# A mixture-of-experts layer: the transposes of a tail's second gated half move behind the main block's down product, and one of the two down weight groups is split into two reduced-precision halves

## The chip, the cores and the metric

The kernel runs on one core of a Trainium2 chip. The metric is the time of one execution in microseconds (us) as the device gives it, the median of several runs. The core has a matrix engine (TensorE, "PE" in the rows, "PEld" its weight loads), a vector engine (VectorE, "DVE"), an activation engine (ScalarE, "ACT"), GpSimd ("POOL") and a queue of transfers ("SP"). Each engine works off its own list of instructions in order, and they wait for each other by semaphores.

## The reference, cut to what matters

The layer is a decoder block: layer norm and modulation, attention and pooling, an output projection, and then a mixture of 16 experts, of which every token uses two. The change touches the experts alone:

```python
def hierarchical_moe(u, w_rg, b_rg, w_re, b_re, w_gate, w_up, w_down):
    ...
    y = jnp.zeros((t, d), jnp.float32)
    for e in range(N_EXPERTS):
        h = jax.nn.silu(u @ w_gate[e]) * (u @ w_up[e])
        y = y + combine[:, e:e + 1] * (h @ w_down[e]).astype(jnp.float32)
    return y.astype(u.dtype)
```

There are 1024 tokens, the model width is 1024 and an expert's hidden width is 512. All is float32.

## The kernel before, in words

The first 560 us are the attention half and the routing. Then the 16 experts follow one another in the program, numbered here by their place, 0 to 15. An expert gathers its tokens by an indirect transfer (`gather`): up to 128 in the main block, and if it has more than 128, up to 64 in a **tail**. Everything for the tail stands in two branches on the count (`tc.If(n_e > P)`, lines 1242 and 1263), which every engine takes or skips by itself. With the inputs at hand the experts at places 2, 4, 6, 8, 10 and 12 have a tail.

The weights of an expert come in six groups of 1 MB, 128 x 4 x 512 float32 (`load_group`): groups 0 and 1 are the first half of the gate and up weights, 2 and 3 the second half, 4 and 5 the down weights. They land in a ring of eleven buffers (`RAW`, whose names in the rows are `raw`, `arena`, `mixT`). For the main block, groups 0 to 3 are **split** (`split_group`): ACT rounds a half group to a reduced-precision float32 (`HR`, line 968) and DVE takes the remainder (`LR`, line 971), two halves per group, into a ring of three slots (`NH`). The tokens are split in the same way (`prep`: PE transposes them at line 998, ACT makes the high part at line 1000, DVE the low part at line 1001, both named `xa`). A product of split operands is three PE passes, high by high, high by low, low by high (`mm_split`, lines 1091 to 1093). `NSP = 4` is the number of groups per expert that are split. As soon as group s has been used, the splitting of group s + 3 is issued.

The main block of an expert: `gate_up(0)` and `gate_up(1)` are 48 passes. Each gives a 128 x 512 sum of gate and up, which `gated` turns into 256 hidden columns (ACT line 1148, DVE line 1149). `turn` transposes these on PE (two transposes, line 1156) and ACT copies them out of PSUM to `hh` (line 1158). The first half a0 is turned in the midst of `gate_up(1)`, the second half a1 after the first branch. `down` multiplies `hh` by the down weights as plain float32, eight matmuls of 128 x 512 (line 1175). `emit` scales the result and `send` adds it to a buffer in memory by an indirect transfer (line 1224).

The tail, in the first branch: its tokens are transposed and copied (`xb`, lines 1007 and 1008), 16 plain float32 matmuls per half on two halves of the array (`gate_up_tail`, line 1097), then `fold` (ACT line 1011, DVE line 1012) and `gated` for the halves b0 and b1, and `turn` for both. The second branch holds the tail's down product and its `emit`.

After the first branch the tokens of the next expert are prepared (`prep(e + 1)`). The transposes of `prep` and of `turn` share two PSUM buffers, `tr`, in turn. A scheduler orders the instructions of each engine, so that the lists of the engines differ somewhat from the order of the source and from expert to expert. The end is the last expert together with a final layer norm (`final`) over the buffer in memory, which can be read only when expert 14 has sent its result.

Of the kernel before, what the change touches and what calls it, by code (L numbers as in the profile page):

```python
# [8 lines left out]
F32 = mybir.dt.float32  # L9
F32R = mybir.dt.float32r  # L10
BF16 = mybir.dt.bfloat16
I32 = mybir.dt.int32
AF = mybir.ActivationFunctionType
# [4 lines left out]
P = 128  # L18
# [3 lines left out]
KC = D // P  # L22
# [8 lines left out]
NE = 16  # L31
NCH = 24
GRP = 4
# [17 lines left out]
WS = "vvvv"  # L51
PRE = 0
SPLIT = 800
NSP = 4
RB = 0
TB = 1
MT = 2
# [28 lines left out]
def row_bcast(ap, n, off=0):  # L86
    return bass.AP(tensor=ap.tensor, offset=ap.offset + off, ap=[[0, P], [1, n]])
# [3 lines left out]
def hybrid_layer(ctx: ExitStack, tc: tile.TileContext, x, c, w_ada, b_ada, w_qk, w_v, w_p, w_pool,  # L91
                 pool_scale, w_out, ln1_g, ln1_b, w_r, b_r, w_moe, ln2_g, ln2_b, eye, out):
    nc = tc.nc
# [35 lines left out]
    def after(a, b, c=mybir.DependencyClass.NoSync):  # L129
        tc.add_manual_dep(b.ins, a.ins.name, mybir.DependencyInfo(c, mybir.DependencyReason.DATA), reason="order")  # L130
# [16 lines left out]
    if True:  # L147
# [369 lines left out]
        for t in range(nfill):  # L517
# [6 lines left out]
            while done < acc:  # L524
                n = next(fill, None)
# [8 lines left out]
        pt = ps.tile([P, 512], F32, name="tr")  # L534
# [18 lines left out]
    g1, b1, sc2, h2, gate1 = (rows[:, r] for r in range(5))  # L553
# [311 lines left out]
    NL, NH = 11, 3  # L865
# [84 lines left out]
    act = moe.enter_context(tc.tile_pool(name="act", bufs=2))  # L950
# [8 lines left out]
    def note(k, ins):  # L959
        newest[k] = ins  # L960
        return ins

    def split_group(s):
        m = NG * (s // NSP) + s % NSP
        r, l, h = RAW[m % NL], LR[s % NH], HR[s % NH]
        for a in range(2):
            cs = slice(2 * a, 2 * a + 2)
            rnd = note("a", nc.scalar.activation(h[:, cs], r[:, cs], AF.Copy))  # L968
            if s == 0:
                after(turned[0], rnd)  # L970
            sub = note("d", nc.vector.tensor_sub(l[:, cs], r[:, cs], h[:, cs]))  # L971
            if s < NH:
                after(ready, sub)
# [3 lines left out]
    def slots(e, b, n):  # L977
        if e < NS:
            return Ti[:n, b * 16 + e, 0:1], T[:n, b * 16 + e, 1:2]
        return TP.bitcast(I32)[:n, b, e - NS, 0:1], TP[:n, b, e - NS, 1:2]  # L980
# [22 lines left out]
    def prep_tail():  # L1003
        for g in range(2):
            pt = ps.tile([P, 4, HB], F32, name="tr")
            for j in range(4):
                nc.tensor.transpose(pt[:, j], XG[2][:HB, (4 * g + j) * P:(4 * g + j + 1) * P], ident[:HB, :HB])
            note("a", nc.scalar.activation(xb[:, 4 * g:4 * g + 4], pt, AF.Copy))
# [63 lines left out]
    def expert(e, n_e):  # L1072
# [9 lines left out]
        xa_h, xa_l = XA[e % 2]  # L1082
        hts = [[], []]

        def raw(g, j):
            return RAW[(NG * e + g) % NL][:, j]

        def mm_split(o, k, s, j):
            tick()
            h, l = HR[s % NH][:, j], LR[s % NH][:, j]  # L1090
            nc.tensor.matmul(o, xa_h[:, k], h, start=k == 0, stop=False)  # L1091
            nc.tensor.matmul(o, xa_h[:, k], l, start=False, stop=False)  # L1092
            nc.tensor.matmul(o, xa_l[:, k], h, start=False, stop=k == KC - 1)  # L1093

        def mm_pair(o, x, w, k, n):
            q = HALF[k % 2]
            nc.tensor.matmul(o[q], x, w, start=k < 2, stop=k >= n - 2)

        def whole_of_ybuf(ins):
            for o in sent[-1]:  # L1100
                after(o, ins, mybir.DependencyClass.Sync)

        def rest(t):
            if not last:
                return
            if t == 0:
                nc.sync.dma_start(gb[:, 0], row_bcast(ln2_g, D))
                nc.sync.dma_start(gb[:, 1], row_bcast(ln2_b, D))
                for i in range(NT):
                    whole_of_ybuf(nc.sync.dma_start(YT[i], ybuf[i * P:(i + 1) * P]))  # L1110
            if t == 1:
                for b in range(2):
                    whole_of_ybuf(nc.gpsimd.indirect_dma_start(
                        out=XG[2 if b else e % 2][:cnts[b]], out_offset=None, in_=ybuf[:],
                        in_offset=bass.IndirectOffsetOnAxis(ap=slots(e, b, cnts[b])[0], axis=0),
                        bounds_check=S - 1, oob_is_err=False))
# [3 lines left out]
        def tick():  # L1120
            ticks[0] += 1
            n = ticks[0] - BS1
            if last and n >= 0 and n % BR1 == 0:
                next(bulk, None)

        def gate_up(half, mid=None):
            pg = ps.tile([P, 512], F32, name="mm", bufs=6)
            for k in range(KC):
                s = NSP * e + 2 * half + k // GRP
                mm_split(pg, k, s, k % GRP)  # L1130
                if mid and k in mid:
                    mid[k]()
                if k % GRP == GRP - 1 and s + NH < NE * NSP:
                    split_group(s + NH)
            return pg

        def gate_up_tail(half):
            pg = ps.tile([P, 512], F32, name="mm", bufs=6)
            for k in range(KC):
                mm_pair(pg, xb[:, k], raw(2 * half + k // GRP, k % GRP), k, KC)  # L1140
            return pg

        def gated(b, pg):
            n = cnts[b]
            s = act.tile([P, 512], F32, name="silut" if b else "silu")[:n]
            if n == HB:
                pg = fold(s, pg)
            note("a", nc.scalar.activation(s[:, :256], pg[:, :256], AF.Silu))
            note("d", nc.vector.tensor_mul(s[:, :256], s[:, :256], pg[:, 256:]))
            return s  # L1150

        def turn(b, s):
            n = cnts[b]
            pt = ps.tile([P, 2, P], F32, name="tr")
            for j in range(2):
                nc.tensor.transpose(pt[:, j, :n], s[:, j * P:(j + 1) * P], ident[:n, :n])
            hh = act.tile([P, 2, P], F32, name="hh", bufs=4)[:, :, :n]
            note("a", nc.scalar.activation(hh, pt[:, :, :n], AF.Copy))
            hts[b].append(hh)

        pys = [[], []]
# [3 lines left out]
        def down(b, g):  # L1165
            for dh in range(2):
                if g == 0:
                    pys[b].append(ps.tile([P, 512], F32, name="mm", bufs=6))
                for f in range(2):
                    k, w = 2 * g + f, raw(4 + g, 2 * f + dh)  # L1170
                    if b:
                        mm_pair(pys[b][dh], hts[b][g][:, f], w, k, 4)
                    else:
                        tick()
                        nc.tensor.matmul(pys[b][dh], hts[b][g][:, f], w, start=k == 0, stop=k == 3)  # L1175
# [4 lines left out]
        def new_y(b):  # L1180
            ys_[b] = ytail if b else act.tile([P, D], F32, name="y", bufs=1)
# [40 lines left out]
        def send(b):  # L1222
            n = cnts[b]
            sc = nc.gpsimd.indirect_dma_start(  # L1224
                out=out if last else ybuf[:], out_offset=bass.IndirectOffsetOnAxis(ap=slots(e, b, n)[0], axis=0),
                in_=ys_[b][:n], in_offset=None, bounds_check=S - 1, oob_is_err=False,
                **({} if last else dict(compute_op=OP.add)))
            for o in stores if last else ():
                after(o, sc, mybir.DependencyClass.Sync)
            for o in sent[-1]:  # L1230
                after(o, sc, mybir.DependencyClass.Sync)
            for o in prev:
                tc.declare_no_dep(sc.ins, o.ins, reason="tokens of one expert are distinct")
            prev.append(sc)

        rest(0)
        pa0 = gate_up(0)
        a0 = gated(0, pa0)
        rest(1)
        pa1 = gate_up(1, {MT: lambda: turn(0, a0)})  # L1240
        a1 = gated(0, pa1)
        with tc.If(n_e > P):
            prep_tail()
            pb0 = gate_up_tail(0)
            b0 = gated(1, pb0)
            pb1 = gate_up_tail(1)
            turn(1, b0)
            b1 = gated(1, pb1)
            turn(1, b1)
        newest.clear()  # L1250
        refill(range(NG * e, NG * e + 4))
        if not last:
            prep(e + 1)
        turn(0, a1)
        down(0, 0)
        down(0, 1)
        new_y(1)
        new_y(0)
# [2 lines left out]
        emit(0)  # L1261
        send(0)
        with tc.If(n_e > P):
            down(1, 0)
            down(1, 1)
            emit(1)
# [5 lines left out]
    def refill(ms):  # L1272
        for m in ms:
            if m + NL < NE * NG:
                load_group(m + NL)
# [64 lines left out]
    with tc.If(top > P + HB):  # L1340
# [8 lines left out]
        e = nc.values_load(perm[0:1, ND - 1:ND], min_val=0, max_val=NE - 1)  # L1349
# [63 lines left out]
```

## Time and profile before

| | us |
|---|---|
| three runs | 1035.01 to 1038.65, median 1037.75 |
| the profiled execution, its own time | 1037.95 |
| its span, from the first to the last instruction | 1036.2 |
| PE busy | 866.7 (84%) |
| DVE busy | 724.6 (70%) |
| ACT busy | 463.3 (45%) |
| mean granted TensorE clock | 0.924 of 2.4 GHz |

Outside the span lie 1.75 us. PE is the busiest engine, but a share of busy time is a mean over stages; the stage that the change touches runs from 567 to 988 us. Matmuls are recorded longer than their distance, since they are pipelined: what a pass costs is read from the starts of the records. A plain float32 matmul leaves two records in the trace, a split pass or a transpose one.

### The profile page before, as it was taken

The page shows a single profiled execution, that of the slowest core. Times are in us where ns is not written, and L with a number is a line of the kernel's source. Part 1 is how long each engine was busy: PE and PEld are TensorE (multiplying, and loading weights), DVE is VectorE, ACT ScalarE, POOL GpSimd, SP SyncE. Part 2 cuts the span into 40 slices and gives each one's busy share as a digit, 9 for nine tenths or more (in the row PEclk, how much of TensorE's full clock was granted, in tenths as well). Part 3 has the DMA queues.
Part 4 walks back from the last instruction along what each step waited for, and adds up shares of the span by engine and source line. Part 5 has one row for each costly group of instructions (what it writes and reads, how often), then busy time and mean ns, then how long its engine had stood idle before and what let it go on. Part 6 is the DMA issues. An engine that isn't in the chain of part 4 may idle for free. (4 is left out here: it accounts for less than half of the span.)

```text
span 1036.2 us, 12860 instructions
## 1 busy us (share of the span) xinstructions
PE 866.7 (84%) x4109; PEld 594.7 (57%) x4110; DVE 724.6 (70%) x1249; ACT 463.3 (45%) x792; POOL 357.7 (35%) x356
## 2 busy tenths in 40 slices
PE   4879888999989798879763999989898999999820
PEld 3658666777767566666642664636455555546510
DVE  7889899787888896968486664735565655647453
ACT  3341544545545654555223553634444544535260
POOL 4775052060134334445463421203020211211383
PEclk7899989999999898999885999999999999999965
DMA  8847533010100522224237697968768787787741
GB/s 307 302 145 247 193 102 102 24 41 24 42 23 21 153 92 82 83 77 174 95 130 293 237 341 251 304 220 269 278 197 322 211 310 222 282 281 265 231 177 63
DMA packets 42467, 186.90 MB, mean 180 GB/s; under 512 B 7921, under 2 KB 8977, under 8 KB 30096
## 3 DMA queue, kind: packets, MB, share of 16 engines
q1 hardware_dynamic: 34608, 168.57, 44.9%
q0 software_dynamic: 7776, 17.33, 7.2%
q8 instruction: 40, 0.66, 0.3%
q14 instruction: 43, 0.35, 0.1%
HBM read 169.19 MB, written 25.33 MB: 188 GB/s over the span
## 5 line engine op out<-in xcount | busy, mean ns | idle before, releaser
L1091 PE MATMUL mm<-HR,xa 128*128 128x512 f32 x256 | 106.9, 418 | 0.1
L988 POOL DMA_INDIRECT V<-u2d,TP x28 | 33.9, 1212 | 209.5 <-issue 85.5
L1092 PE MATMUL mm<-LR,xa 128*128 128x512 f32 x256 | 102.2, 399 | 0.1
L1093 PE MATMUL mm<-HR,xa 128*128 128x512 f32 x256 | 100.4, 393 | 0.1
L971 DVE TENSOR_TENSOR LR<-raw,HR 128x1024 fp32r<-128x1024 f32 x56 | 68.4, 1224 | 19.6 <-ACT HR L968 16.8
L968 ACT ACTIVATE HR<-raw 128x1024 fp32r<-128x1024 f32 x56 | 59.3, 1061 | 49.2 <-PE mm L1093 48.8
L422 PE MATMUL mm<-AT,V 128*64 128x128 f32 x576 | 60.2, 313 | 24.1 <-ACT AT L413 11.6
L971 DVE TENSOR_TENSOR LR<-mixT,HR 128x1024 fp32r<-128x1024 f32 x50 | 61.1, 1224 | 18.7 <-ACT HR L968 15.6
L968 ACT ACTIVATE HR<-mixT 128x1024 fp32r<-128x1024 f32 x50 | 53.0, 1061 | 45.9 <-PE mm L1093 45.7
L471 PE MATMUL mm<-uh,wh 128*128 128x512 f32 x160 | 70.9, 443 | 3.1 <-ACT V L315 1.9
L473 PE MATMUL mm<-uh,wl 128*128 128x512 f32 x160 | 65.4, 409 | 1.9 <-DVE wl L170 1.9
L422 PEld LDWEIGHTS mm<-AT,V 128*64 128x64 f32 x576 | 42.2, 154 | 42.9 <-ACT AT L413 16.8
L472 PE MATMUL mm<-ul,wh 128*128 128x512 f32 x160 | 65.0, 406 | 0.0
L383 DVE TENSOR_TENSOR_SCAN N<-N,zcol 128x767 f32<-128x767 f32 (+7 forms) x45 | 59.4, 1321 | 6.7 <-ACT N L377 6.2
L444 POOL TENSOR_TENSOR mixT<-pT 128x344 f32<-128x344 f32 (+1 forms) x12 | 14.3, 1204 | 131.2 <-ACT pT L432 131.2
L1175 PE MATMUL mm<-raw,hh 128*128 128x512 f32 x112 | 58.1, 650 | 0.4
L1091 PEld LDWEIGHTS mm<-HR,xa 128*128 128x128 f32 x256 | 48.6, 190 | 13.9 <-issue 3.3
L1092 PEld LDWEIGHTS mm<-LR,xa 128*128 128x128 f32 x256 | 48.6, 190 | 13.2 <-issue 4.1
L1093 PEld LDWEIGHTS mm<-HR,xa 128*128 128x128 f32 x256 | 48.4, 189 | 10.6 <-issue 0.8
L410 PE MATMUL tr<-ident,arena 128*128 128x128 f32 x288 | 46.2, 284 | 8.0 <-DVE L L728 6.2
L1220 DVE SCALAR_TENSOR_TENSOR y<-mm,TP,sg 128x512 f32<-128x512 f32 x26 | 19.5, 750 | 38.4 <-PE mm L1175 35.7
L377 ACT ACTIVATE N<-zz 128x767 f32<-128x767 f32 (+7 forms) x45 | 28.2, 627 | 39.1 <-DVE zz L376 38.8
(375 smaller groups left out, 2226.2 us busy)
## 6 DMA issues: line engine op xcount, KB each, us to landing
raw<-in_w_moe_dram SPq DMA_DIRECT2D x42, 1024.0 KB, 7.7
mixT<-in_w_moe_dram SPq DMA_DIRECT2D x36, 1024.0 KB, 8.8
arena<-in_w_moe_dram SPq DMA_DIRECT2D x18, 1024.0 KB, 7.8
arena<-in_w_ada_dram SPq DMA_DIRECT2D x24, 512.0 KB, 4.3
wada<-in_w_ada_dram SPq DMA_DIRECT2D x12, 512.0 KB, 5.9
mixT<-in_w_ada_dram SPq DMA_DIRECT2D x12, 512.0 KB, 3.5
ybuf<-sg SPq DMA_DIRECT2D x8, 512.0 KB, 2.6
wraw<-in_w_qk_dram SPq DMA_DIRECT2D x6, 512.0 KB, 4.0
```

The costliest lines, as they stand in the source:

```text
L383: nc.vector.tensor_tensor_scan(N[:, 1:nk], N[:, 1:nk], zcol.to_broadcast([P, nk - 1]), 1.0, op0=OP.mult, op1=OP.add)
L410: nc.tensor.transpose(pt[:, j], E[:, (g + j) * P:(g + j + 1) * P], ident)
L422: nc.tensor.matmul(po[h * HD:(h + 1) * HD, :P], V[:, cp, i + j, h * HD:(h + 1) * HD], ST[cp, i, h][j // 4][:, j % 4], start=j == 0, stop=j ...
L471: nc.tensor.matmul(po, h[:, k], uh[:, k, cs], start=k == 0, stop=False)
L472: nc.tensor.matmul(po, h[:, k], ul[:, k, cs], start=False, stop=False)
L473: nc.tensor.matmul(po, l[:, k], uh[:, k, cs], start=False, stop=k == KC - 1)
L968: rnd = note("a", nc.scalar.activation(h[:, cs], r[:, cs], AF.Copy))
L971: sub = note("d", nc.vector.tensor_sub(l[:, cs], r[:, cs], h[:, cs]))
L1091: nc.tensor.matmul(o, xa_h[:, k], h, start=k == 0, stop=False)
L1092: nc.tensor.matmul(o, xa_h[:, k], l, start=False, stop=False)
L1093: nc.tensor.matmul(o, xa_l[:, k], h, start=False, stop=k == KC - 1)
L1175: nc.tensor.matmul(pys[b][dh], hts[b][g][:, f], w, start=k == 0, stop=k == 3)
```

## The change

`NSP` becomes 5: group 4, the first of the two down groups, is split for the main block as well. The first half a0 goes to a new tile `hs` with a high part (ACT) and a low part (DVE), and the four matmuls of `down(0, 0)` become four times three split passes; `down(0, 1)` stays plain float32, as does the tail's whole down product. The splitting of the group three places on is issued behind `down(0, 0)` too. `turn(1, b1)` leaves the first branch and stands at the head of the second, behind the main block's down product. `rest(1)`, which acts in the last expert only, moves behind the first branch.

```diff
-NSP = 4
+NSP = 5
...
-        def mm_split(o, k, s, j):
+        def mm_split(o, xh, xl, s, j, first, end):
             tick()
             h, l = HR[s % NH][:, j], LR[s % NH][:, j]
-            nc.tensor.matmul(o, xa_h[:, k], h, start=k == 0, stop=False)
-            nc.tensor.matmul(o, xa_h[:, k], l, start=False, stop=False)
-            nc.tensor.matmul(o, xa_l[:, k], h, start=False, stop=k == KC - 1)
+            nc.tensor.matmul(o, xh, h, start=first, stop=False)
+            nc.tensor.matmul(o, xh, l, start=False, stop=False)
+            nc.tensor.matmul(o, xl, h, start=False, stop=end)
+
+        def split_ahead(s):
+            if s + NH < NE * NSP:
+                split_group(s + NH)
...
-            hh = act.tile([P, 2, P], F32, name="hh", bufs=4)[:, :, :n]
-            note("a", nc.scalar.activation(hh, pt[:, :, :n], AF.Copy))
+            if b == 0 and not hts[0]:
+                hh = act.tile([P, 2, 2, P], F32R, name="hs")
+                note("a", nc.scalar.activation(hh[:, 0], pt, AF.Copy))
+                note("d", nc.vector.tensor_sub(hh[:, 1], pt, hh[:, 0]))
+            else:
+                hh = act.tile([P, 2, P], F32, name="hh", bufs=4)[:, :, :n]
+                note("a", nc.scalar.activation(hh, pt[:, :, :n], AF.Copy))
...
+                    elif g == 0:
+                        hs = hts[0][0]
+                        mm_split(pys[0][dh], hs[:, 0, f], hs[:, 1, f], NSP * e + 4, 2 * f + dh, k == 0, False)
...
-        rest(1)
         pa1 = gate_up(1, {MT: lambda: turn(0, a0)})
...
             b1 = gated(1, pb1)
-            turn(1, b1)
         newest.clear()
+        rest(1)
...
         down(0, 0)
+        split_ahead(NSP * e + 4)
         down(0, 1)
...
         with tc.If(n_e > P):
+            turn(1, b1)
             down(1, 0)
```

How the lists of the engines change is seen on PE at two places. Line numbers shift: 1242 becomes 1253, 1263 becomes 1275, 1156 becomes 1160, 1175 becomes 1187. In these rows `Activation_49` and the like are the counters of the engines that an instruction waits for. First PE's list before, in expert 7 (which has no tail), from the end of the first branch to the second and past it:

```order
L1242 UNCONDITIONAL_BRANCH [waits PE_49]
L1175 MATMUL mm<-mixT,hh 128x512 [waits DMAHW5_49,Activation_49]
L998 MATMUL tr<-ident,V 128x128 [waits DMASW5_49,PE_49,Activation_49]
L998 MATMUL tr<-ident,V 128x128 x3
L998 MATMUL tr<-ident,V 128x128 [waits PE_49,Activation_49]
L998 MATMUL tr<-ident,V 128x128 x3
L1175 MATMUL mm<-mixT,hh 128x512 x2
L1263 COMPARE_AND_BRANCH
```

The same place in PE's list of the changed kernel:

```order
L1253 UNCONDITIONAL_BRANCH [waits PE_49]
L1091 MATMUL mm<-HR_4593,hs 128x512 [waits Activation_49]
L998 MATMUL tr<-ident,V 128x128 [waits DVE_49,DMASW5_49,PE_49,Activation_49]
L998 MATMUL tr<-ident,V 128x128 x3
L998 MATMUL tr<-ident,V 128x128 [waits PE_49,Activation_49]
L998 MATMUL tr<-ident,V 128x128 x3
L1092 MATMUL mm<-LR_4590,hs 128x512
L1093 MATMUL mm<-HR_4593,hs 128x512
L1160 MATMUL tr<-ident,silu 128x128 [waits DVE_49]
L1160 MATMUL tr<-ident,silu 128x128
L1091 MATMUL mm<-HR_4593,hs 128x512
L1275 COMPARE_AND_BRANCH
```

One split pass stands ahead of the transposes of `prep` where one plain matmul stood, and the transposes of a1 (line 1160), which stood behind the second branch, now stand two passes behind those of `prep`. Places 5, 7, 9, 11 and 13 are alike in this; at the even places from 4 on, five passes stand between instead of two, at places 1 to 3 eleven, at place 0 twelve.

Second, the tail of expert 8 in PE's list before, from the end of the tail's gate and up product (`silut` is a half of the tail):

```order
L1097 MATMUL mm<-raw_4586,xb 64x512 x3
L1156 MATMUL tr<-ident,silut 128x64 [waits DVE_49,PE_49]
L1156 MATMUL tr<-ident,silut 128x64
L1156 MATMUL tr<-ident,silut 128x64 [waits DVE_49,PE_49]
L1156 MATMUL tr<-ident,silut 128x64
L1242 UNCONDITIONAL_BRANCH
```

And in the changed kernel the head of the second branch of the same expert:

```order
L1275 COMPARE_AND_BRANCH
L1160 MATMUL tr<-ident,silut 128x64 [waits DVE_49,PE_49]
L1160 MATMUL tr<-ident,silut 128x64
L1101 MATMUL mm<-raw_4587,hh 64x512 [waits DMAHW3_49]
L1101 MATMUL mm<-raw_4587,hh 64x512 x3
L1101 MATMUL mm<-raw_4588,hh 64x512 [waits DMAHW4_49,Activation_49]
```

The second pair of transposes, those of b1, has left the first branch and stands ahead of the tail's down product.

## Rows read from the trace of the kernel before

**Rows 1.** Busy time of each engine in two stretches, then clock, DMA share, GB/s.

```profile
640.00:680.00 40.00, 38.65 (x160) 25.21 (x160) 27.22 (x29) 20.89 (x28) 9.67 (x7) 1.00 0.79 258
1000.00:1036.20 36.20, 0.00 (x0) 0.00 (x0) 13.90 (x19) 7.11 (x13) 16.44 (x23) 0.50 0.19 74
```

**Rows 2.** Who waited for whom, 590 to 985 us: total us, times, longest.

```profile
PE tr L1156 <- DVE silut L1149: 12.8, 6, 2.1
PE mm L1097 <- ACT xb L1008: 5.5, 6, 1.1
...
SPq L875 <- PE mm L1175: 112.4, 27, 12.0
...
SPq L1110 <- DMA ybuf<-y,TP: 13.5, 1, 13.5
```

**Rows 3.** Timeline of PE in expert 3: start, duration; 27 passes lie between these starts.

```profile
646.04 0.39 PE L1091 MATMUL mm<-HR,xa 128*128 128x512 f32 x1
...
652.16 0.39 PE L1091 MATMUL mm<-HR,xa 128*128 128x512 f32 x1
```

**Rows 4.** Timeline of expert 7, from the first branch to its end.

```profile
770.07 1.10 PE L1175 MATMUL mm<-mixT,hh 128*128 128x512 f32 x2 [0.30 <-PEq L1242]
770.77 0.36 ACT L1148 ACTIVATE silu<-mm 128x256 f32<-128x256 f32 x1
771.23 0.86 PEld L998 LDWEIGHTS tr<-ident,V 128*128 128x128 f32 x8 [0.90 <-ACTq L1242]
...
771.93 1.08 ACT L1000 ACTIVATE xa<-tr 128x512 fp32r<-128x512 f32 x2 [0.80 <-PE tr L998]
...
772.17 1.88 PE L1175 MATMUL mm<-mixT,hh 128*128 128x512 f32 x4
772.60 1.29 DVE L1001 TENSOR_TENSOR xa<-tr,xa 128x512 fp32r<-128x512 f32 x2
...
774.44 4.46 PE L1175 MATMUL mm<-mixT,hh 128*128 128x512 f32 x10
...
778.34 0.79 PE L1091 MATMUL mm<-HR,xa 128*128 128x512 f32 x1
```

**Rows 5.** Timeline of expert 4: the halves of the tail, and a1.

```profile
683.91 0.34 PE L1156 MATMUL tr<-ident,silut 64*128 64x64 f32 x2
...
685.37 0.42 ACT L1148 ACTIVATE silut<-silut 64x256 f32<-64x256 f32 x1 [0.44 <-DVE silut L1012]
685.82 0.42 DVE L1149 TENSOR_TENSOR silut<-silut 64x256 f32<-64x256 f32 x1 [0.48 <-ACT silut L1148]
686.16 0.41 DVE L1149 TENSOR_TENSOR silu<-silu,mm 128x256 f32<-128x256 f32 x1
...
686.38 0.30 PE L1156 MATMUL tr<-ident,silut 64*128 64x64 f32 x2 [2.13 <-DVE silut L1149]
```

**Rows 6.** Timeline of PE: turning of b0, and next expert's first pass, experts 8 and 10.

```profile
798.79 0.34 PE L1156 MATMUL tr<-ident,silut 64*128 64x64 f32 x2
...
813.23 0.80 PE L1091 MATMUL mm<-HR,xa 128*128 128x512 f32 x1
...
853.99 0.34 PE L1156 MATMUL tr<-ident,silut 64*128 64x64 f32 x2
...
870.11 0.79 PE L1091 MATMUL mm<-HR,xa 128*128 128x512 f32 x1
```

**Rows 7.** Busy time and granted clock behind that wait, experts 4 and 8.

```profile
687.00:691.00 4.00, 4.00 (x12) 2.12 (x11) 1.38 (x2) 1.20 (x3) 1.05 (x1) 0.57 1.01 416
...
801.40:806.00 4.60, 4.54 (x20) 2.25 (x21) 1.29 (x2) 1.36 (x3) 1.05 (x1) 1.00 0.99 415
```

**Rows 8.** Costliest groups: line, engine, names, shapes, count; busy us, mean ns; idle before.

```profile
L971 DVE TENSOR_TENSOR LR<-raw,HR 128x1024 fp32r<-128x1024 f32 x56 | 68.4, 1224 | 19.6 <-ACT HR L968 16.8
L968 ACT ACTIVATE HR<-raw 128x1024 fp32r<-128x1024 f32 x56 | 59.3, 1061 | 49.2 <-PE mm L1093 48.8
```

**Rows 9.** Timeline of PE in expert 5, behind the first branch.

```profile
713.43 1.10 PE L998 MATMUL tr<-ident,V 128*128 128x128 f32 x8 [1.46 <-ACTq L1242]
```

More of the change, by code (lines that the diff above doesn't have):

```diff
@@ L1129, in gate_up @@
                 s = NSP * e + 2 * half + k // GRP
-                mm_split(pg, k, s, k % GRP)
+                mm_split(pg, xa_h[:, k], xa_l[:, k], s, k % GRP, k == 0, k == KC - 1)
                 if mid and k in mid:
                     mid[k]()
-                if k % GRP == GRP - 1 and s + NH < NE * NSP:
-                    split_group(s + NH)
+                if k % GRP == GRP - 1:
+                    split_ahead(s)
             return pg
```

## The prediction, as it was made before the changed kernel ran

> **What bounds the kernel now.** I read first the table of stretches, then the list of who waited for whom, then the timeline of single experts. In the expert stage PE is busy 38.7 of 40 us, DVE 27.2 and ACT 20.9 [rows 1]: PE sets the pace, and a saving counts only if PE starts its next work sooner. The end of the program is another matter. After 1000 us PE does nothing [rows 1]; the transfers for the final layer norm wait for the scatter of expert 14's result [rows 2]. So what is saved up to the end of expert 14 reaches the end, and what expert 15 saves on PE does not, since its product is ready long before the norm needs it. Weight transfers are no bound: SP waits 112 us for PE to release buffers [rows 2], not PE for SP, and a buffer is asked for a whole expert ahead.
>
> In the waits of PE itself two lines stand out [rows 2]: six times 2.13 us for the tail's b1 (the transposes wait for DVE's product), and six waits, five of 1.05 us and a short one, for `xb`.
>
> **The work that becomes shorter.** Twenty-seven split passes take 6.12 us, 0.227 us each [rows 3]; three are 0.68. Ten records of plain float32, five matmuls, run from 774.44 to 778.74 [rows 4] (the next expert's first record starts at 778.34 while the last matmul still runs, and is 0.79 instead of 0.39 long, so I count the end 0.40 later, here and below): 0.86 us each. Four products go from 0.86 to 0.68, 0.72 us an expert, 10.8 us for fifteen. The Trainium skill, page "TensorE: Matmul & The Clock Gate", section "Back-to-back issue gap", gives 518 cycles for 512 columns, an estimate of 0.216 us a pass, by which four products would save 0.85 us and fifteen experts 12.8; the trace shows 0.227, and I go by the trace.
>
> **The added splitting.** Per expert ACT gets two roundings of 1.06 us and DVE two subtractions of 1.22 [rows 8], and DVE the low part of `hs`. That operation is not in the trace: below it is 0.41, a 128x256 operation that reads PSUM [rows 5], above it 0.65, half of the pair of 1.29 on 128x512 [rows 4]; I take 0.41, which has its size. DVE gets 2.9 us an expert. Two experts without a tail fill the 40 us of [rows 1], where DVE then works 33 us and ACT 25. The cover: a half group is used in six passes, 1.36 us, and costs DVE 1.22, and two groups always lie ready, 5.4 us of PE work. I cost it at nothing; if that cover were gone each expert would pay up to 2.9 us.
>
> **What eats the gain in experts without a tail.** Behind the first branch the transposes of `prep` wait for ACT's counter, and ACT passes the branch only after a1's silu. In expert 7 that silu ends at 771.13 and the transposes start at 771.23 [rows 4]. Before, a plain matmul of 0.86 fills most of that wait; now one pass of 0.23 stands there, and the transposes cannot start earlier. The bounds of the added idle are 0 and 1.46 us, what expert 5 shows with nothing in front [rows 9]; I take 0.63. Then a second wait, which was hidden: the transposes of a1 need the PSUM buffer that `prep`'s first half leaves when DVE has made its low part, the first half of the pair of 1.29 from 772.60, so at 773.27 [rows 4]. Before, two plain matmuls and the branch covered this (the transposes of a1 came at 774.2). Now two passes cover 0.45, from 772.17 to 772.62.
>
> The walk for expert 7: transposes of a1 at 773.34, done 773.58; four passes 774.49; a skipped branch 0.15; five passes 775.77; four plain matmuls 779.21. Before it was 778.74 [rows 4]. So experts 7, 9, 11 and 13, with the same order, lose 0.46 each, 1.8 us. Expert 14 has five passes in front of a1's transposes, which cover the wait: it gains 0.2. In expert 5 the long wait is there already, and eight plain matmuls follow it: 7.51 from transposes to end plus 0.86 before, 7.98 after, a gain of 0.4. Expert 0 keeps its order and gains the 0.7. In experts 1 and 3 the last six gate-up passes stood behind the branch, so that ACT was through in time; now they stand ahead of it. They get the 1.46 and a branch of 0.15 for two gaps of 0.3, less 0.72: a loss of 0.3 each. Sum: 1.8 - 0.2 - 0.4 - 0.7 + 0.6 = 1.1 us lost.
>
> **What the tails gain.** Take time from the turning of b0. Before, expert 8 needs 813.63 - 798.79 = 14.84 us to its end [rows 6]. After, DVE's list is the limit: a1's product ends 2.66 us after the turning of b0 [rows 5], `prep`'s first low part 0.65 later at 3.3, and a1's transposes start at about 3.4 (PE would be ready at 2.7: two pairs of transposes, a pass, then five). What stands behind: transposes 0.24; two passes 0.45; transposes of b1 0.24 and a branch, 0.3 together; four passes 0.91; four plain matmuls 3.44; and the tail's down product, 16 records of 0.222, 3.55. The sum is 12.3, a gain of 2.5 us: 0.7 for the passes and 1.8 of the 2.13. So experts 4, 6, 8, 10 and 12 gain 12.5. Expert 2 has its wait for `xb` near nothing now, since six gate-up passes stand behind the branch there too; it gets the 1.05 that the others have and saves 3.0 by eleven passes as cover: 2.2. Together 14.7.
>
> **The clock.** Behind the 2.13 us wait the granted clock was 0.57 in expert 4, between PE's levels of 1.2 and 2.4 GHz, with only 12 records in 4 us; in expert 8 it was 1.00 [rows 7]. Experts 6 and 10 look like the first row, 2 and 12 like the second. The price is in [rows 6]: from the turning of b0 expert 10 needs 16.12 us to the next record, expert 8 14.44, so 1.68 more. After the change the longest wait there is 0.7 us, and I take the three falls as gone: 5.0 us. But experts 7, 9, 11 and 13 now idle about 2.0 us within 3.6 us, in three pieces (0.30, 0.93 and 0.7). Nothing in the trace is quite like it: a single wait of 1.46 fell nowhere, waits of 2.13 fell in three of six. Bounds are 0 and four falls; I take one, 1.7 us.
>
> **The sum.** 1.1 - 14.7 - 5.0 + 1.7 = -16.9 us on the profiled execution's own 1037.95, which lies 0.2 above the median: 1021.0.
>
> **Where else it could go.**
> Absorbed nowhere: every expert keeps its 0.72, the tails lose all of 2.13, no clock falls: 10.8 + 12.8 + 5.0 less 0.8 for expert 2's `xb` wait is 27.8, so 1010. For it speaks that scheduled lists have hidden such waits before; against it the fixed start at 771.23 in [rows 4].
> The clock falls at the new idle: four falls instead of one, 1026; if the old three stay too, 1031.
> The turning of b1 was not what held PE: prep's transposes and a1's need the same two PSUM buffers and the same ACT and DVE lists as the tail's silu, so the 2.13 could reappear there in full. Without the tails' 1.8 each (10.8 for six) and the clock, 16.9 becomes 1.1, so 1037; with the clock recovered 1032. Against it [rows 5]: DVE is through with a1 0.2 us after PE's old wait ends, and `prep` no longer follows it.
> Slower: DVE becomes the bound. Its list is in order, a late subtraction of the down group stands in front of a1's product, and PE waits for that product. If all of the 2.9 us lands on PE in fifteen experts, 43 us are paid, and the time is about 1064; it decides from 1.1 us an expert on (16.9 / 15). Against it: ACT, not DVE, is what DVE mostly waits for (16.8 of 19.6 us before these subtractions [rows 8]).
>
> **How the numbers follow.** The forecast has 0.55 (1016 to 1026, 1021 its middle), absorbed nowhere 0.08, the clock 0.17, the tails' wait kept 0.12, DVE 0.08. The measurement cannot tell 0.3%, 3.1 us, from no change. Faster than 1034.6 are the first three and half of the fourth: 0.86; same 0.08, the rest of the fourth and a mild form of the last; slower 0.06. For 8 in 10 the range leaves out most of "nowhere" and the slow ends: 1013 to 1031.
>
> **What would show each step.** In the profile after: `hs` passes 0.227 apart; no wait of the tail's transposes for DVE's `silut`; a granted clock of 1.00 behind the tails' gate and up product; expert 8 ending 12.3 us after the turning of b0; in experts 7 to 13 without a tail, waits of `prep`'s transposes for ACT of about 0.9 us and of a1's transposes for DVE of about 0.7, and a period of 20.7 to 20.8 instead of 20.3. Wrong would be: a wait of split passes for `LR`, experts without a tail gaining 0.7, or clocks below 1 in them.

## The result, and the profile after

The changed kernel takes 1020.75 us (median of four runs, 1019.73 to 1022.9) beside 1036.45 for the kernel before: ratio 0.985, interval 0.982 to 0.988. The forecast was 1021.0.

The profiled execution after took 1019.73 us, 18.2 less than that of before. I follow this difference through one instruction that has the same place in both lists, the turning of a0 (two transposes in the midst of the second gate and up product). Here it is in experts 0 and 14, then the scatter of expert 14's result, in PE's and POOL's timelines before:

```profile
579.52 0.38 PE L1156 MATMUL tr<-ident,silu 128*128 128x128 f32 x2
...
954.51 0.39 PE L1156 MATMUL tr<-ident,silu 128*128 128x128 f32 x2
...
967.64 1.56 POOL L1224 DMA_INDIRECT ybuf<-y,TP  x1 [4.32 <-DVE y L1220]
```

And after:

```profile
577.77 0.38 PE L1160 MATMUL tr<-ident,silu 128*128 128x128 f32 x2
...
936.89 0.40 PE L1160 MATMUL tr<-ident,silu 128*128 128x128 f32 x2
...
950.17 1.56 POOL L1236 DMA_INDIRECT ybuf<-y,TP  x1 [4.43 <-DVE y L1232]
```

Between the two turnings lie 374.99 us before and 359.12 after, 15.87 less. From the second one to the scatter it is 13.13 and 13.28. So the stage that the change touches gives 15.7 us, as much as the medians differ. The other 2.6 us of the profiled pair lie outside it: 1.75 had been won before expert 0 turned a0, where PE's list is the same, and 0.83 behind the scatter. I put them down to these two executions and not to the change: in the ten profiles of this document expert 0 turns a0 between 574.6 and 581.8 us, and 66.7 to 69.3 us lie behind the scatter.

Who waited for whom, 590 to 985 us, after (total us, times, longest); it answers to [rows 2]:

```profile
PE tr L1160 <- DVE xa L1001: 5.9, 11, 0.8
...
PE mm L1101 <- ACT xb L1008: 5.5, 6, 1.1
...
PE tr L998 <- ACTq L1253: 5.1, 6, 0.8
...
PE tr L1160 <- DVE silu L1153: 2.1, 1, 2.1
...
PE tr L998 <- PEq L1253: 0.9, 2, 0.5
```

The six waits of 2.13 us for the tail's b1 are gone. In their place stand two new ones, for ACT's counter in front of `prep`'s transposes (0.84 in the odd experts from 5 on and in 14; expert 0, which turns a0 before 590 us, has had its own of 0.8 before and after) and for DVE's low part of `xa` in front of those of a1 (0.55 in the odd experts, 0.4 to 0.8 in the tails). The wait of 2.1 is in expert 15 and off the path; the two of 0.4 to 0.5 for PE's own sequencer are in experts 1 and 3.

Expert 7 after, in the timeline of all engines; it answers to [rows 4]:

```profile
754.87 0.39 PE L1160 MATMUL tr<-ident,silu 128*128 128x128 f32 x2
...
757.96 0.47 PE L1091 MATMUL mm<-HR,hs 128*128 128x512 f32 x1
...
758.81 0.37 ACT L1152 ACTIVATE silu<-mm 128x256 f32<-128x256 f32 x1
...
759.27 1.09 PE L998 MATMUL tr<-ident,V 128*128 128x128 f32 x8 [0.84 <-ACTq L1253]
...
760.64 1.29 DVE L1001 TENSOR_TENSOR xa<-tr,xa 128x512 fp32r<-128x512 f32 x2
...
761.38 0.44 PE L1160 MATMUL tr<-ident,silu 128*128 128x128 f32 x2 [0.55 <-DVE xa L1001]
...
762.35 0.39 PE L1091 MATMUL mm<-HR,hs 128*128 128x512 f32 x1
762.89 0.47 PE L1092 MATMUL mm<-LR,hs 128*128 128x512 f32 x1
...
767.15 0.79 PE L1091 MATMUL mm<-HR,xa 128*128 128x512 f32 x1
...
775.95 0.40 PE L1160 MATMUL tr<-ident,silu 128*128 128x128 f32 x2
```

From `prep`'s transposes to those of a1 it is 2.11 us, the number of the walk. From there to the end (767.15 + 0.40) it is 6.17, where the walk has 5.87. The period, from 754.87 to 775.95, is 21.08; before it was 20.33:

```profile
766.85 0.40 PE L1156 MATMUL tr<-ident,silu 128*128 128x128 f32 x2
...
787.18 0.40 PE L1156 MATMUL tr<-ident,silu 128*128 128x128 f32 x2
```

Expert 8 after, from the turning of b0; it answers to [rows 5, 6]:

```profile
787.58 0.34 PE L1160 MATMUL tr<-ident,silut 64*128 64x64 f32 x2
...
789.83 0.41 DVE L1153 TENSOR_TENSOR silu<-silu,mm 128x256 f32<-128x256 f32 x1
...
790.16 1.27 DVE L1001 TENSOR_TENSOR xa<-tr,xa 128x512 fp32r<-128x512 f32 x2
790.89 0.44 PE L1160 MATMUL tr<-ident,silu 128*128 128x128 f32 x2 [0.42 <-DVE xa L1001]
...
791.72 0.33 PE L1160 MATMUL tr<-ident,silut 64*128 64x64 f32 x2
791.98 3.65 PE L1101 MATMUL mm<-raw,hh 128*64 128x512 f32 x16
...
799.62 0.79 PE L1091 MATMUL mm<-HR,xa 128*128 128x512 f32 x1
```

The product of a1 ends 2.66 us after the turning of b0, its transposes start at 3.31, and the end (799.62 + 0.40) is at 12.44. b1 is turned at 791.72 without any wait.

Busy time and granted clock after: a stretch that answers to [rows 1], and then what follows the transposes of a1 in the tails of experts 4 and 10, where [rows 7] had 0.57 and [rows 6] a late end.

```profile
640.00:680.00 40.00, 38.39 (x172) 25.61 (x170) 30.62 (x33) 23.54 (x31) 12.13 (x7) 1.00 0.80 260
...
683.60:687.60 4.00, 4.00 (x20) 1.66 (x22) 0.48 (x1) 0.73 (x3) 0.19 (x1) 1.00 0.99 417
...
844.50:848.50 4.00, 4.00 (x20) 1.65 (x22) 0.46 (x1) 0.74 (x3) 0.17 (x1) 1.00 1.00 420
```

DVE works 30.6 of 40 us instead of 27.2, and no fall of the clock is left: nine stretches of 40 us from 600 to 960 all show 1.00.

### The profile page after: what moved, and what is told of

Same layout as the page of the kernel before. It is cut to its first block, busy times and chain, and to the rows that moved or that the text cites. A ratio compares the mean times of both kernels' runs of the same rounds, so it can differ in the third digit from the quotient of the medians.

```text
span 1017.9 us, 13116 instructions
## 1 busy us (share of the span) xinstructions
PE 852.6 (84%) x4173; PEld 603.1 (59%) x4174; DVE 766.0 (75%) x1297; ACT 493.8 (49%) x824; POOL 369.3 (36%) x356
## 5 line engine op out<-in xcount | busy, mean ns | idle before, releaser
L971 DVE TENSOR_TENSOR LR<-raw,HR 128x1024 fp32r<-128x1024 f32 x70 | 85.0, 1223 | 26.3 <-ACT HR L968 22.7
L968 ACT ACTIVATE HR<-raw 128x1024 fp32r<-128x1024 f32 x70 | 73.4, 1059 | 43.5 <-PE mm L1093 38.0
L971 DVE TENSOR_TENSOR LR<-mixT,HR 128x1024 fp32r<-128x1024 f32 x62 | 75.5, 1224 | 18.5 <-ACT HR L968 13.5
L968 ACT ACTIVATE HR<-mixT 128x1024 fp32r<-128x1024 f32 x62 | 65.2, 1058 | 38.7 <-PE mm L1093 38.3
L1236 POOL DMA_INDIRECT ybuf<-ytail,TP x13 | 30.4, 2335 | 54.8 <-DVE ytail L1230 47.3
L347 ACT ACTIVATE qs<-q 64x128 fp32r<-64x128 f32 x64 | 19.7, 308 | 55.8 <-PE zz L363 55.2
```

## The experiments

My theory behind the forecast: the gain is that of the tails, by the moved turning of b1 and the clock that falls no more; the shorter down product earns little, since two waits that it used to hide come out. The rival: the shorter passes earn it (10.8 us).

The results in one table. "Stage" is the time between the turnings of a0 in experts 0 and 14, less 374.99 of before; the next three columns split it into the six periods with a tail, those of experts 5, 7, 9, 11 and 13, and those of 0, 1 and 3. In both_split a0 is turned two passes later than elsewhere from expert 5 on, which makes 0.5 us of its stage, in the period of expert 4.

| kernel | median us | ratio to before, interval | stage | six tails | 5 to 13 | 0, 1, 3 |
|---|---|---|---|---|---|---|
| changed kernel | 1020.75 | 0.985 (0.982 to 0.988) | -15.9 | -18.5 | +2.9 | -0.3 |
| move_only | 1018.0 | 0.982 (0.980 to 0.984) | -17.2 | -18.6 | +0.8 | +0.6 |
| split_only | 1037.1 | 1.000 (0.999 to 1.002) | +0.2 | +1.4 | -0.1 | -1.1 |
| down_first | 1011.9 | 0.978 (0.975 to 0.980) | -23.5 | -20.1 | -4.1 | +0.7 |
| plain_first | 1015.5 | 0.981 (0.980 to 0.983) | -18.3 | -17.9 | -0.9 | +0.5 |
| tr_three | 1022.8 | 0.988 (0.985 to 0.990) | -15.3 | -15.7 | +1.1 | -0.7 |
| both_split | 1024.8 | 0.990 (0.988 to 0.992) | -13.5 | -11.1 | -5.7 | +3.3 |
| prep_second | 1072.5 | 1.038 (1.034 to 1.042) | +31.9 | +4.3 | +16.7 | +11.0 |
| rest_back | 1020.3 | 0.985 (0.983 to 0.987) | -15.8 | -18.4 | +2.9 | -0.3 |

The medians come from three groups of runs, in which the kernel before had 1036.45 (the changed kernel), 1037.55 (move_only, split_only, down_first, tr_three) and 1035.64 (the others), so the ratios are to be compared.

**move_only: the moved turning alone.** The kernel before with this edit:

```diff
             b1 = gated(1, pb1)
-            turn(1, b1)
...
         with tc.If(n_e > P):
+            turn(1, b1)
             down(1, 0)
```

> The kernel before with one edit: the turning of b1 stands at the head of the second branch. NSP stays 4, no down group is split. Theory (the tails carry the gain): the six waits of 2.13 us for the tail's product are gone, 12.8 us, and the three falls of the clock behind them, 5.0 us, so 17.8 less than 1036.45: 1018.6, between 1014 and 1023, with a granted clock of 1.00 in every stretch from 600 to 960 us. Experts without a tail keep their period of 20.3 us. Rival (the shorter passes carry the gain): only the clock comes back, 5 us, and the time is 1031 or more. Second rival (the 2.13 us only move to another wait): no wait for silut, but a wait of about 2 us for xb, xa or silu in the same experts, and 1032 to 1037.

It is 1.8% faster than before. The six tails gain 18.6 us, as much as in the changed kernel with its split. The waits, 590 to 985 us:

```profile
PE tr L998 <- ACTq L1242: 1.5, 1, 1.5
...
PE tr L1156 <- DVE xa L1001: 0.8, 1, 0.8
```

No wait for `silut` is left. The one for ACT is that which expert 5 had before [rows 9], and a single one for `xa` has come. Experts 7 to 13 without a tail take 20.5 us, not the 20.3 expected: behind the second branch PE's idle time is 0.30 instead of 0.15. The granted clock is 1.00 in every stretch of 40 us from 600 to 960. The move and the clock carry the whole gain; both rivals fall.

**split_only: the split alone.** The changed kernel, with the turning of b1 put back:

```diff
             b1 = gated(1, pb1)
+            turn(1, b1)
...
         with tc.If(n_e > P):
-            turn(1, b1)
             down(1, 0)
```

> The changed kernel with one part undone: the turning of b1 is back in the first branch, the first down group stays split. Theory (the tails carry the gain): the six waits of 2.13 us are there again, with falls of the clock at about three of them (0 to 6, 1.7 us each). Six experts with a tail gain 0.72 each, 4.3 us. In experts 5 to 13 without a tail five passes instead of two stand here in front of the transposes of a1, so only the first of the two new waits is left and they lose about 0.2 each, 1.0 us; the first experts gain 1.0 together. Sum 4.3 less than 1036.45: 1032, between 1027 and 1037 with the clock. Rival (the shorter passes carry the gain): 10.8 us less, 1025.6, or fewer.

No change at all: 1.000, where I expected 4.3 us and the rival 10.8. The six waits of 2.13 are there again. Granted clock behind them, at places 2, 4, 6, 8, 10 and 12 (busy times of PE, PEld, DVE, ACT and POOL, clock, DMA share, GB/s):

```profile
630.00:635.00 5.00, 4.12 (x17) 3.23 (x17) 1.97 (x3) 2.72 (x6) 1.41 (x1) 0.70 0.99 410
...
690.00:695.00 5.00, 5.00 (x21) 3.69 (x22) 1.38 (x2) 1.86 (x4) 1.05 (x1) 0.66 0.89 344
...
745.00:750.00 5.00, 3.60 (x21) 2.57 (x23) 1.71 (x3) 2.04 (x5) 1.05 (x1) 1.00 0.97 387
...
800.00:805.00 5.00, 3.77 (x18) 2.72 (x19) 1.71 (x3) 2.17 (x5) 1.05 (x1) 0.76 1.00 415
...
855.00:860.00 5.00, 2.87 (x14) 2.46 (x14) 1.12 (x3) 2.10 (x5) 0.00 (x0) 0.72 0.97 387
...
915.00:920.00 5.00, 4.48 (x23) 1.91 (x23) 1.29 (x2) 1.13 (x3) 1.05 (x1) 1.00 0.92 354
```

The clock fell at four places of six. Even the two tails in which it did not (periods 34.70 and 34.80, undisturbed ones of before 34.88 and 34.92) gained 0.1 to 0.2 instead of 0.72, since a1's transposes wait there for DVE's low part of `xa`, 0.5 us each. Expert 2 lost 4.8: DVE scales the tail's result there (638.94 to 641.70) before it makes the low part of `xa`, a1's transposes wait 2.26 us for that, and the clock falls a second time. That and the other falls make up the rest of what I missed.

**down_first: both waits covered.** The changed kernel in another order:

```diff
-        if not last:
-            prep(e + 1)
-        turn(0, a1)
         down(0, 0)
+        turn(0, a1)
+        if not last:
+            prep(e + 1)
         split_ahead(NSP * e + 4)
         down(0, 1)
```

> The changed kernel in another order behind the first branch: the split down product of a0 first (12 passes, 2.7 us), then the turning of a1, then the preparation of the next tokens, then the plain down product of a1. Theory (two new waits eat the shorter passes in experts without a tail): both waits have 2.7 us of passes in front of them now. Those of prep for ACT (5.1 us in 590 to 985) and of a1 for DVE (5.9) go, and 1.0 in expert 0: 12 less than 1020.75, 1009, between 1006 and 1013; experts without a tail take 19.6 to 19.8 us instead of 21.1. Rival (DVE's longer list sets the pace): the same idle time appears at another place of PE, with DVE as the releaser, and the time stays within 3 us of 1020.75.

The fastest of all kernels here, 2.2% below before. Both waits are gone in expert 7, whose timeline goes on where 12 split passes have begun at 758.02:

```profile
754.94 0.39 PE L1160 MATMUL tr<-ident,silu 128*128 128x128 f32 x2
...
758.55 0.39 PE L1093 MATMUL mm<-HR,hs 128*128 128x512 f32 x1
...
760.65 0.39 PE L1093 MATMUL mm<-HR,hs 128*128 128x512 f32 x1
761.00 0.41 PE L1160 MATMUL tr<-ident,silu 128*128 128x128 f32 x2
761.25 1.29 PE L998 MATMUL tr<-ident,V 128*128 128x128 f32 x8
...
774.61 0.40 PE L1160 MATMUL tr<-ident,silu 128*128 128x128 f32 x2
```

The period is 19.67, 1.41 less than in the changed kernel, which is the sum of its two waits, 0.84 and 0.55. So these two waits ate the shorter product. It did not reach 1009: in experts 0, 2 and 4 the transposes of a1 now wait 1.2 us for DVE's product (in expert 2 a rounding on ACT stands in front of the silu of a1), and in expert 3 the transposes of `prep` wait 1.0.

**plain_first: that order without a split.** The edit of down_first, made in move_only.

> The order of down_first without any split of down groups (NSP is 4): plain float32 product of a0 first, then the turning of a1, the preparation of the next tokens, the product of a1; b1 is turned in the second branch. Theory (the split is worth its 0.72 an expert only where the waits are covered): 7 to 11 more than down_first, 1021, between 1018 and 1024; experts without a tail at 20.3 to 20.4 us, no wait of prep's transposes for ACT, none of a1's for xa. Rival (the order alone does it and the split is worth nothing in any order): within 2 us of 1011.9.

Experts 5 to 13 without a tail take 20.3 us as expected, and down_first's 19.7 are 0.64 less; with a tail it is 32.70 against 32.08. So the covered split is worth about 0.63 an expert there, and that is all that its passes save: in the list of down_first nine of them lie between the starts at 758.55 and 760.65, 0.233 us each and not 0.227, so that four products save 4 x 0.86 - 12 x 0.233 = 0.64 and not 0.72. The time, 1015.5, is below the range that I expected and above the rival's: it is 0.4% above down_first by the two ratios and not 0.9%, for in places 0 to 4 the split loses 0.5 in all, by the waits just named. The two intervals overlap a little, so what the covered split is worth rests on the traces.

**tr_three: a third buffer.** The changed kernel with this edit, by which the transposes of a1 come directly behind those of `prep`:

```diff
-    ps = ctx.enter_context(tc.tile_pool(name="ps2", bufs=2, space=PSUM))
+    ps = ctx.enter_context(tc.tile_pool(name="ps2", bufs=3, space=PSUM))
...
-            pg = ps.tile([P, 512], F32, name="mm", bufs=6)
+            pg = ps.tile([P, 512], F32, name="mm", bufs=5)
```

> The changed kernel with three PSUM buffers for transposes instead of two (and five instead of six for products). The scheduler then puts the transposes of a1 directly behind those of prep. Theory (the second new wait is for the buffer that prep's first half leaves): the transposes of a1 no longer wait for DVE's low part of xa but for DVE's product of a1. In experts without a tail that product ends 1.2 us after the start of prep's transposes, which take 0.95: a wait of about 0.3 instead of 0.55. In tails it ends 2.66 us after the turning of b0, and PE is ready at about 1.6: a wait of 1.1 instead of 0.4. Sum: 1.4 gained, 3.8 lost, 1023, between 1019 and 1026. Rival (the wait is not for a buffer): the wait of a1's transposes for xa stays, 0.5 us or more in experts without a tail.

The waits, 590 to 985 us:

```profile
PE tr L1160 <- DVE silu L1153: 9.2, 8, 2.9
...
PE tr L1160 <- DVEq L1253: 0.9, 5, 0.2
```

No wait for `xa` is left: the second new wait was for the PSUM buffer. What remains in experts without a tail is five waits of 0.18; in tails the wait is now for the product of a1, 1.0 us each in the mean (0.64 to 1.27), and they lose 2.8 against the changed kernel. The time, 1022.8, is the 1023 of the expectation.

**both_split: DVE's load raised further.** From down_first, with `NSP = 6` and all of the main block's down product split:

```diff
-            if b == 0 and not hts[0]:
+            if b == 0:
...
-                    elif g == 0:
-                        hs = hts[0][0]
-                        mm_split(pys[0][dh], hs[:, 0, f], hs[:, 1, f], NSP * e + 4, 2 * f + dh, k == 0, False)
                     else:
-                        tick()
-                        nc.tensor.matmul(pys[b][dh], hts[b][g][:, f], w, start=k == 0, stop=k == 3)
+                        hs = hts[0][g]
+                        mm_split(pys[0][dh], hs[:, 0, f], hs[:, 1, f], NSP * e + 4 + g, 2 * f + dh, k == 0, k == 3)
...
         down(0, 1)
+        split_ahead(NSP * e + 5)
```

> The order of down_first, and both down groups split (NSP is 6): no plain float32 product is left in the main block. Theory (with the waits covered, a shorter product is worth its 0.72 us an expert): up to 10.8 less than the 1011.9 of down_first, 1001; since the first experts there already showed waits behind ACT's and DVE's longer lists, 1004, between 999 and 1009, experts without a tail at about 19.0 us. Rival (DVE becomes the bound): two more subtractions of 1.22 and a low part of 0.42 make DVE's work about 35 of 39 us; if its list sets the pace, split passes wait for LR, or the transposes of a1 for DVE's product, and the time is 1012 or more.

Here the rival holds: 1.3% slower than down_first by the two ratios. The timeline of expert 7, where PE turns a0:

```profile
755.64 0.39 ACT L1152 ACTIVATE silu<-mm 128x256 f32<-128x256 f32 x1
...
756.97 2.34 DVE L971 TENSOR_TENSOR LR<-mixT,HR 128x1024 fp32r<-128x1024 f32 x2
...
759.24 0.41 DVE L1153 TENSOR_TENSOR silu<-silu,mm 128x256 f32<-128x256 f32 x1
...
759.70 0.44 PE L1160 MATMUL tr<-ident,silu 128*128 128x128 f32 x2 [1.78 <-DVE silu L1153]
```

ACT has the silu at 756.03. Its product on DVE comes at 759.24, behind subtractions that are late, and PE waits 1.8 us; it is so in each of experts 5, 7, 9, 11 and 13, and with 1.2 and 1.7 us in 3 and 4. The wait stands in front of the turning, so the table has it in the period before, that of the tails (33.7 instead of 32.1 us); the experts without a tail behind it take 19.37 us, 0.3 less than in down_first and not the 19.0 expected. It is not DVE's share of busy time that decides: it is 34.0 of 40 us from 800 to 840, where such waits stand, and more in a stretch in which PE has no such wait:

```profile
920.00:960.00 40.00, 38.99 (x174) 29.64 (x173) 37.16 (x43) 29.71 (x36) 10.80 (x7) 1.00 0.77 248
```

What costs here is a late list, worked off in order.

**prep_second: the first wait covered, the second one's cover taken away.** The changed kernel with `down(0, 0)` moved in front of `prep(e + 1)`, and `turn(0, a1)` directly behind that:

```diff
+        down(0, 0)
         if not last:
             prep(e + 1)
         turn(0, a1)
-        down(0, 0)
```

> The changed kernel with 12 split passes in front of prep's transposes and none between those and the transposes of a1. Theory (two separate waits, each as long as its cover is short): the wait of prep's transposes for ACT is gone; that of a1's transposes for DVE's low part of xa comes in every expert, 1.0 to 1.2 us (2.1 us after prep's start, less 0.95 of transposes). Against the changed kernel experts without a tail gain 0.3, tails lose 0.7, the first ones lose 1.4 together: 4 more, 1025, between 1021 and 1029. Rival (one wait, for a1's gate product): a1's transposes wait for silu, or not at all, and the time is about that of down_first, 1012.

It is 3.8% slower than before, far beyond what I expected. The wait for `xa` comes as named, but 2.6 to 3.2 us long. The timeline of expert 7:

```profile
782.57 1.03 PE L998 MATMUL tr<-ident,V 128*128 128x128 f32 x8
783.17 2.36 DVE L971 TENSOR_TENSOR LR<-raw,HR 128x1024 fp32r<-128x1024 f32 x2 [0.93 <-ACT HR L968]
783.98 1.07 ACT L1000 ACTIVATE xa<-tr 128x512 fp32r<-128x512 f32 x2
...
785.44 1.28 DVE L1001 TENSOR_TENSOR xa<-tr,xa 128x512 fp32r<-128x512 f32 x2
786.18 0.44 PE L1160 MATMUL tr<-ident,silu 128*128 128x128 f32 x2 [2.58 <-DVE xa L1001]
```

ACT's next two roundings, released by a split pass of `down(0, 0)`, and DVE's two subtractions stand in front of `xa` in the two lists. The wait was the one named, and its price was 1.4 to 2 us an expert too low. The clock falls too: all nine stretches from 600 to 960 show 0.91 to 0.96.

**rest_back: the smallest part undone.** `rest(1)` stands ahead of `gate_up(1)` again.

```diff
         a0 = gated(0, pa0)
+        rest(1)
...
         newest.clear()
-        rest(1)
```

> The changed kernel with the smallest part undone: rest(1), the last expert's gathers, stands in front of the second gate and up product again. Theory: nothing, within 3 us of 1020.75, since what ends last are the stores of the final norm, not these gathers. Rival: the gathers come in the way of the transfers for the norm, 2 us or more later.

0.985 as with the change: the move of `rest(1)` is worth nothing that can be measured.

## Why the prediction was right, and which of its steps were not

**What bounds the kernel.** That a saving in the expert stage reaches the end, and one in expert 15 does not, is what the two scatters show: 15.7 us in the stage, 15.7 in the medians.

**The tails.** The walk for expert 8 gave 12.3 us, the trace 12.44. Experts 4, 6 and 10 were to gain 4.2 with the clock and gained 4.04 to 4.11; 8 and 12 were to gain 2.5 and gained 2.41 and 2.16. Expert 2 gained 1.67 instead of 2.2, and not by the step that I gave: its wait for `xb` stayed at 0.2, and a1's transposes wait 0.79 there. ACT's list shows why `xb` comes in time: in expert 4 a rounding (671.55) and a1's silu (672.51) stand in front of the copy of `xb` (672.78), in expert 2 neither does (619.97). In sum 18.5 instead of 19.7.

**The two new waits.** They are what I named, by the releaser in the rows and by down_first, which removes them and gains their sum, and by tr_three, which removes the second alone. Their sizes were 0.93 and 0.7 in the forecast, 0.84 and 0.55 in the trace. All the same the odd experts from 7 on lose 0.75, not 0.46: between the turnings of a1 and the end the walk is 0.30 short. Half of that is the skipped second branch: between the starts at 762.35 and 762.89 lie 0.54, of which a pass is 0.23, so the branch costs 0.31. I took 0.15, the idle time that rows show in front of the instruction behind a branch; counted from start to start, as I counted the passes, it is 0.31 in the kernel before too (773.46 to 774.20, of which a plain record is 0.43). The Trainium skill, page "Advanced Engine Details and Errata", section "Control Flow Timing", has about 51 ns for a branch and 108 for a compare-and-branch, together an estimate of 0.16; the trace shows 0.15 as idle time and 0.31 from start to start. The rest is in two steps between passes that take 0.31 to 0.32 instead of 0.23, the first behind the transposes (761.58 to 761.89) and the first behind the branch (762.89 to 763.19). Four passes lie between a1's transposes and the branch, as the walk has it; of them the list in the section on the change shows only one. In experts 1 and 3 I took 1.46 for the first wait; it is 0.4 to 0.5 and not for ACT, whose silu of a1 comes only after the transposes there (600.87 and 600.35 in expert 1), and they gain 0.2 to 0.3 instead of losing 0.3. Expert 0, which was to gain 0.7 by keeping its order, lost 0.2 (0.41 between the turnings, of which 0.23 is one pass by which expert 1 now turns a0 later): a1's transposes have come to wait 0.24 for `xa` there, and the plain product behind them 0.15 for ACT; what makes up the rest is open.

**The clock.** Three falls gone, as forecast. The one new fall that I charged (1.7) did not come: two waits of 0.84 and 0.55 in one expert cost nothing of the clock.

**The sum.** Without the new fall my terms give -18.6; the stage gave -15.7. The fall charged for nothing covered 1.7 of that miss of 2.9, which is 1.2 in experts 7 to 13, 1.2 in the tails and 0.4 in the others together: expert 0 came out 0.9 worse than forecast and 5 and 14 together 0.6 worse, 1 and 3 together 1.0 better. The rest is covered by the runs of before, whose median is 1.3 lower here than in the three shown. So the number is nearer than its terms, and that is luck.

**DVE.** Its 33 us were worked out as if the 40 us of [rows 1] held two experts without a tail. They hold expert 3 and parts of 2 and 4, tails among them, and after the change DVE works 30.6 there. No split pass waits for `LR`, as forecast; the low part of `hs` takes 0.42, where I took 0.41.

**What the split is worth.** My terms gave the shorter passes 4.2 in the tails against 1.1 lost elsewhere. move_only says that in this order they lose 1.3 in the stage (the timed intervals of the two overlap, so this rests on the traces), and split_only that alone they gain nothing. The step that failed is "0.7 for the passes and 1.8 of the 2.13": move_only's tails gain as much as those of the changed kernel, so the full 2.13 goes by the move and a little more (2.46 and 2.51 in experts 8 and 12, where no clock had fallen), and the passes give nothing in a tail of this order. There a1's transposes wait 0.4 to 0.8 us for `xa`, which in move_only they do in expert 2 alone. A second term was too large as well: passes with `hs` stand 0.233 us apart, so the shorter product is worth 0.64 an expert at most and not 0.72. DVE as the bound, the slower rival, was not met by this change but by the next step of the same kind, both_split.

## What to carry to other kernels

A shorter product next to a wait is worth only what other work covers: look up which wait ends last behind it, and put independent work there first; with `down(0, 0)` in front, the same split earned about 0.63 us an expert, by the traces, that it had lost in the order of the change. When a change has two parts, run each alone: here one part carries all, and the total hides that the other costs a little by the traces (1.3 us in the stage). An engine far from full can still set the pace, if a late instruction stands in front of one that is waited for.

## What the runs showed of the hardware that I had not expected

The granted clock fell behind waits of 2.13 us in three of six cases before and in four of six in split_only, and behind none of the waits of 1.8 us and less (both_split, down_first and tr_three show 1.00 in all stretches from 600 to 920). The length of a wait did not decide it alone: in expert 15 of tr_three PE waits 2.85 us, up to 967.0, and the clock stays at 1.00 from 964 to 976. A fall cost 1.7 us in the kernel before (periods of 36.59 and 34.90), in split_only 0.8 to 1.0 (35.5 to 35.8 and 34.75).

A branch that is skipped moves PE's next matmul back by 0.31 us, whether it parts two split passes (starts 0.54 apart instead of 0.23, in the changed kernel) or two plain records (0.74 instead of 0.43, in down_first), though the rows show only 0.15 of it as idle time. In move_only it is 0.46 (0.89 apart), with 0.30 as idle time.
